# Encoder block on one core: bias products over 128 rows, the two last banks added by halves in turns, and sums moved in VectorE's queue

## The chip, the cores and the metric

The kernel runs on one core of a Trainium2 chip. The metric is the time of one execution on the device, in microseconds (us); less is better. The executions shown are few, so the median is given with the lowest and the highest. One further execution was recorded by the profiler, and all rows quoted below come from that one.

## The reference

The kernel computes one encoder block for one sequence of 256 tokens with 2048 channels in float32. Three token mixers (A: six heads of dilated windows with a relative bias; B: grouped queries with rotary positions; C: cross-attention into 256 memory tokens) run beside each other on one projection, each is sent through its own matrix and gated, and the sum goes through an output projection. A feed-forward part with 5632 hidden channels follows.

```python
h = rms_norm(x, g_mix)
qa, ka, va, qb, kb, vb, qc, gt = split(h @ w_in)
# per dilation group: scores + rel_bias[t5_bucket(rel)] inside the window, NEG outside
oa = mixture of the three dilated groups, by their softmax denominators
ob, oc = grouped-query attention, cross-attention into rms_norm(mem)
merged = sigmoid(gt)[0]*(oa @ w_br_a) + sigmoid(gt)[1]*(ob @ w_br_b) + sigmoid(gt)[2]*(oc @ w_br_c)
x = x + merged @ w_o
hf = rms_norm(x, g_ffn) @ w_ffn_in
return x + (silu(hf[..., :D_FF]) * hf[..., D_FF:]) @ w_ffn_out
```

## The kernel before

**Products.** Tokens stand in two tiles of 128 (t = 0, 1). A float32 product is made of three float32r matmuls: each weight chunk (128x1024, called `raw`, `more` or `both` after the place where SyncE's DMA put it) is rounded by ScalarE to `whi` (L457), VectorE subtracts to get the rest `wlo` (L468), and TensorE adds x_hi·whi, x_hi·wlo and x_lo·whi into one PSUM bank of 128x512. The three names occur in this order in the rows, so a late `wlo` holds TensorE at the second matmul of a group. In the queue of an engine instructions run strictly in order.

**Blocks.** Behind the attention, `pair` multiplies two column blocks at a time by a scheme with seven block products in place of eight; the banks are called X, Y, V, W and Q after their products. It needs sums of weight chunks (VectorE, L593 to L599 and L662 to L666), sums of banks (L636, L640) and sums of token tiles (`forms`, and for a single chunk `glone` and `lone`). The strings `STEPS_...` list the order of the steps; a step is one chunk, "." gives a turn to nothing. `run` issues each chunk's products four chunks behind its halves.

**Side jobs.** Everything that is not a product (attention, gating, transposes, stores) is a generator in a list; `tick`, called after each step, moves at most one job that is due, and `hold(n, ...)` starts a job n ticks later. An instruction handed to `nc.follow` keeps its place in program order on its engine; matmuls and SyncE's DMAs always do; for the others a scheduler, which plays the program through in its own model of time, decides the order within an engine. So a moved job moves instructions on VectorE, and in the attention part the scheduler may place everything anew when one operation changes its shape.

**Places that the change touches.** `biases` (L406 to L437) makes the tables of the relative bias: a one-hot table of 33 used rows, padded to 64, is loaded (`oneh`), copied to float32r (`ones`), and multiplied with the bias values repeated over columns (`rep`, split to `reps`): three times two matmuls `bias_ps`, with 64 rows of contraction. It runs beside the projections of the attention heads (`product`, names `mm`). `merging` is the stage that gates the branches; in its first pair `lone_of_gates` (L963 on) builds the token sum `glone` on VectorE and ScalarE, and `merge` (its products are L1002) multiplies a branch's two banks with their gates. `feeding` is the feed-forward part; `output` (its sums are L1123) adds banks to x and stores them. The last column block of all is added in halves of 256 columns: token tile 0 (bank mmY) first gets all its products, then token tile 1 (bank mmX) gets its products for the first half of the columns, then for the second half.

Of the kernel before, what the change touches and what calls it, by code (L numbers as in the profile page):

```python
# [104 lines left out]
def encoder_block(ctx: ExitStack, tc: tile.TileContext, a: dict, out: bass.AP):  # L105
# [271 lines left out]
    def constants():  # L377
# [3 lines left out]
        nc.sync.dma_start(out=rope, in_=a["rope"])  # L381
        nc.vector.memset(relb[:64], NEG)
        nc.sync.dma_start(out=relb[:BUCKETS], in_=a["rel_bias"])
# [22 lines left out]
    def biases():  # L406
# [5 lines left out]
        for g in range(3):  # L412
            oneh, ones = s4([P, NC], "oneh"), s4([P, NC], "ones", F32R)
            nc.sync.dma_start(out=oneh[:64], in_=a["onehot"][:, g])
            yield 3
            nc.scalar.activation(ones[:64], oneh[:64], AF.Copy)
            rep = small.tile([P, P], F32, name="rep", bufs=1)
            reps = small.tile([P, 2, P], F32R, name="reps", bufs=1)
            for i in range(2):
                nc.vector.tensor_copy(rep[:64, 64 * i:64 * i + 64],  # L420
                                      relb[:64, 2 * g + i:2 * g + i + 1].to_broadcast([64, 64]))
            ps = bank("bias_ps")
            split(reps[:64, 0], reps[:64, 1], rep[:64])
            for i in range(2):
                nc.tensor.matmul(ps, lhsT=reps[:64, i], rhs=ones[:64], start=(i == 0), stop=(i == 1))
            row = s4([P, RELS], "row")
# [43 lines left out]
    def pair(src, lhs, lists, done, doubles=(), forms=None, operand=None, fresh="", early=False, by_halves=None, single=None):  # L470
# [51 lines left out]
        def whole(u, c):  # L522
            def ready():
# [15 lines left out]
                def products():  # L539
                    halved = by_halves is not None and c == 0 and left[ends[0][1]] == 2  # L540
                    for i in range(2 * T):
                        t, k = (i % T, i // T) if parts == 2 else (i // 2, i % 2)
                        st = at(2 * u + k, t)
                        if not (halved and t):
                            mul(ends[c][t], st, hi[:, k], lo[:, k], parts == 2)
                    for i in range(4 * halved):
                        if i == 2:
                            with tc.high_priority():
                                by_halves([ps[b] for b in ends[0]])
                        st, k = at(2 * u + i % 2, 1), i % 2  # L550
                        mul(ends[0][1], st, hi[:, k], lo[:, k], cols=slice(i // 2 * NC // 2, (i // 2 + 1) * NC // 2),
                            whole_half=i % 2 == 1)
                    ending()
# [409 lines left out]
    def lone_of_gates():  # L963
        yield 18
        to = lone["gate"] = s8([P, 1, 2, 4, P], "glone", pool=tail)
        one, tl = s4([P, 1, 4, P], "ffull"), xT.tiles[2].bitcast(F32)
        nc.vector.tensor_add(one[:, 0].rearrange("p (k t) s -> p k (t s)", t=T), tl[:, :2, 0], tl[:, :2, 1])
        yield 2
        token_sums(one, to)

    def merging():
# [5 lines left out]
        for b, (g0, k0, k1) in enumerate(((0, 0, 2), (8, 2, 6), (4, 6, 12))):  # L977
            for j in (0, 2) if b else (2,):
                sg, br = {}, {}

                def gates(c, r, j=j, b=b, sg=sg, br=br):
                    sg[c] = s4([P, T, NC], "sg")
                    for t in range(T):
                        nc.scalar.activation(sg[c][:, t], r[t], AF.Sigmoid, scale=r_x[:, 0, t:t + 1])
                    if c in br:
                        start(hold(11 if b < 2 else 0, merged(c, [br[c][:, t] for t in range(T)], j, b, sg)))

                def branch(c, r, j=j, b=b, sg=sg, br=br):
                    if c in sg:
                        return merge(c, r, j, b, sg)  # L990
                    br[c] = s4([P, T, NC], "br")
                    for t in range(T):
                        nc.scalar.activation(br[c][:, t], r[t], AF.Copy)

                def merged(c, r, j, b, sg):
                    merge(c, r, j, b, sg, nc.follow if b < 2 else lambda ins: None)
                    yield 1

# [88 lines left out]
    def feeding():  # L1087
        for c0, c1 in ((0, 4), (4, 8), (8, KF // 4)):
# [25 lines left out]
            for n in (0, 2):  # L1114
                def output(c, r, n=n, last=last, first=False):
                    final = last and n == 2 and c == 0
                    w = NC // 2 if final else NC
                    for t in range(T):
                        for h in range(NC // w):
                            if final and first != (t + h < 2):  # L1120
                                continue
                            o = slice((n + c) * NC + h * w, (n + c) * NC + (h + 1) * w)
                            nc.vector.scalar_tensor_tensor(x[t][:, o], r[t][:, h * w:(h + 1) * w],  # L1123
                                                           r_f[:, 0, t:t + 1], x[t][:, o],
                                                           op0=ALU.mult, op1=ALU.add)
                            if last:
                                start(hold(1 if n else 4, store(t, o)))

                yield pair(lambda u, c, n=n, c0=c0: a["w_ffn_out"][n + c][2 * c0 + u], hTl, pairs[n // 2], output,
                           TWO, by_room(lambda: room), by_halves=(lambda r, f=output: f(0, r, first=True)) if last and n == 2 else None)  # L1130

# [19 lines left out]
def _onehot():  # L1151

    m = np.zeros((64, 3, NC), np.float32)
    for g, (radius, dil) in enumerate(DILS):
# [67 lines left out]
```

## Time and profile before

| | |
|---|---|
| median of 3 executions | 1356.69 us (1356.67 to 1357.27) |
| the profiled execution's own time | 1357.38 us |
| its span (first to last instruction) | 1355.6 us |
| granted TensorE clock | 1.00 |
| busy: TensorE matmul, VectorE, ScalarE | 99%, 87%, 64% |
| mean busy share of the DMA engines over 40 slices | between 0.2 and 0.9 |

A row of the timeline gives the start (us from the span's start), the time taken, engine, line, operation, output<-inputs, how many equal ones were merged, and in brackets how long the engine had been idle and what ended that. PE is TensorE's matmuls, PEld its weight loads, DVE VectorE, ACT ScalarE. Ends of matmuls are modelled: one 128x512 matmul is shown with 0.39 us, while the next one starts about 0.23 us after it. So TensorE's lost time is read from the distance between starts, not from the busy share.

### The profile page before, as it was taken

The numbers are of one execution on the slowest core, as the hardware profiler recorded it, in microseconds if no ns is written. First come the engines' busy times: TensorE is split into PE (matmuls) and PEld (weight loads), VectorE is DVE, ScalarE is ACT, GpSimd is POOL, SyncE is SP. The second block draws the span as 40 slices with busy tenths as digits, with TensorE's granted clock in tenths as the row PEclk, the third lists the DMA queues.
The fourth block names the chain that finished last, engine by engine and source line by source line (L and its number), as shares of the span: only waits on it lengthen the run. The fifth ranks groups of instructions, "written<-read, shape, count | busy, mean of one in ns | idle before, by whom it ended". The sixth has DMA issues, their size and how long they took to land.

```text
span 1355.6 us, 17347 instructions
## 1 busy us (share of the span) xinstructions
PE 1348.8 (99%) x6156; PEld 1117.9 (82%) x6156; DVE 1176.5 (87%) x1458; ACT 864.7 (64%) x1136; POOL 53.1 (4%) x60
## 2 busy tenths in 40 slices
PE   9999999999999999999999999999999999999998
PEld 7888888888888888888888888888888888888887
DVE  6869877768989879889999998988999888989997
ACT  7877665655666656657766666655667655566663
POOL 0010000000000000000000000000000000000000
PEclk9999999999999999999999999999999999999999
DMA  9976445558495584775568766678666787666872
GB/s 371 346 232 217 144 154 177 165 164 285 187 308 161 174 302 155 281 248 167 190 218 264 242 193 221 209 255 276 191 216 210 240 264 219 220 224 206 279 217 94
DMA packets 86344, 301.19 MB, mean 222 GB/s; under 512 B 9777, under 2 KB 12337, under 8 KB 86001
## 3 DMA queue, kind: packets, MB, share of 16 engines
q1 hardware_dynamic: 79488, 275.94, 57.4%
q0 software_dynamic: 6624, 24.12, 9.6%
q8 instruction: 48, 0.79, 0.2%
q14 instruction: 40, 0.32, 0.1%
q10 hardware_dynamic: 144, 0.02, 0.0%
HBM read 297.17 MB, written 2.88 MB: 221 GB/s over the span
## 4 chain that ended last, share of the span: by engine, by line
PE 96%; DVE 3%; issue 0%; ACT 0%; DMA 0%; SPq 0%; DVEq 0%; ACTq 0%
PE mmX L80 28%; PE mmW L80 20%; PE mm L80 17%; PE mmY L80 15%; PE mmQ L80 11%; DVE wlo L468 2%; PE tp L80 1%; PE sc L80 1%; PE o L80 1%; PE pT L80 1%; PE mmV L80 1%; PE hT L80 0%; DVE raw L666 0%; DMA raw<-in_w_mem 0%; DVE x L1123 0%
## 5 line engine op out<-in xcount | busy, mean ns | idle before, releaser
L457 ACT ACTIVATE whi<-raw 128x1024 fp32r<-128x1024 f32 (+1 forms) x354 | 361.4, 1036 | 218.6 <-DVE raw L666 50.4
L468 DVE TENSOR_TENSOR wlo<-raw,whi 128x1024 fp32r<-128x1024 f32 (+1 forms) x354 | 418.4, 1194 | 65.1 <-ACT whi L457 61.1
L80 PE MATMUL mm<-whi,xT 128*128 128x512 f32 x640 | 201.3, 392 | 0.0
L457 ACT ACTIVATE whi<-both 128x1024 fp32r<-128x1024 f32 (+1 forms) x117 | 117.9, 1015 | 62.1 <-PE mmQ L80 21.9
L468 DVE TENSOR_TENSOR wlo<-both,whi 128x1024 fp32r<-128x1024 f32 (+1 forms) x117 | 136.1, 1170 | 22.6 <-ACT whi L457 21.6
L457 ACT ACTIVATE whi<-more 128x1024 fp32r<-128x1024 f32 (+1 forms) x103 | 106.7, 1038 | 55.0 <-DVE more L664 18.1
L133 DVE TENSOR_TENSOR wlo<-raw,whi 128x1024 fp32r<-128x1024 f32 x82 | 103.1, 1261 | 41.1 <-ACT whi L133 36.3
L80 PEld LDWEIGHTS mm<-whi,xT 128*128 128x128 f32 x640 | 119.3, 188 | 23.4
L468 DVE TENSOR_TENSOR wlo<-more,whi 128x1024 fp32r<-128x1024 f32 (+1 forms) x103 | 123.2, 1198 | 13.5 <-ACT whi L457 12.8
L133 ACT ACTIVATE whi<-raw 128x1024 fp32r<-128x1024 f32 x82 | 87.0, 1062 | 61.6 <-PE mm L80 49.5
L80 PE MATMUL mm<-wlo,xT 128*128 128x512 f32 x320 | 125.6, 392 | 0.0
L80 PE MATMUL mmW<-whi,forms 128*128 128x512 f32 x368 | 122.0, 390 | 0.0
L80 PE MATMUL mmX<-whi,forms 128*128 128x512 f32 x368 | 122.0, 390 | 0.0
L80 PE MATMUL mmX<-whi,x1T 128*128 128x512 f32 x352 | 120.9, 389 | 0.0
L80 PE MATMUL mmY<-whi,x1T 128*128 128x512 f32 x264 | 89.1, 389 | 0.0
L80 PEld LDWEIGHTS mmW<-whi,forms 128*128 128x128 f32 x368 | 69.1, 188 | 14.2
L80 PEld LDWEIGHTS mmX<-whi,forms 128*128 128x128 f32 x368 | 69.1, 188 | 14.2
L80 PEld LDWEIGHTS mmX<-whi,x1T 128*128 128x128 f32 x352 | 66.1, 188 | 13.7
L80 PE MATMUL mmX<-wlo,forms 128*128 128x512 f32 x184 | 71.8, 390 | 0.2 <-DVE wlo L468 0.2
L80 PE MATMUL mmW<-wlo,forms 128*128 128x512 f32 x184 | 71.6, 389 | 0.0
L80 PEld LDWEIGHTS mm<-wlo,xT 128*128 128x128 f32 x320 | 60.1, 188 | 12.4 <-issue 0.7
L80 PE MATMUL mmX<-wlo,x1T 128*128 128x512 f32 x176 | 68.5, 389 | 0.0
(311 smaller groups left out, 2602.0 us busy)
## 6 DMA issues: line engine op xcount, KB each, us to landing
raw<-in_w_ffn SPq DMA_DIRECT2D x109, 512.0 KB, 7.4
raw<-in_w_qkv SPq DMA_DIRECT2D x64, 512.0 KB, 4.2
raw<-in_w_gate SPq DMA_DIRECT2D x58, 512.0 KB, 5.2
raw<-in_w_ffn_out SPq DMA_DIRECT2D x53, 512.0 KB, 7.1
both<-in_w_ffn SPq DMA_DIRECT2D x34, 512.0 KB, 6.2
more<-in_w_ffn SPq DMA_DIRECT2D x33, 512.0 KB, 6.4
both<-in_w_gate SPq DMA_DIRECT2D x24, 512.0 KB, 8.3
raw<-in_w_o SPq DMA_DIRECT2D x24, 512.0 KB, 5.8
```

Of the source, the lines that this page charges most:

```text
L80: ins = op(*args, **kw)
L133: ins = [nc.scalar.activation(hi, src, AF.Copy), nc.vector.tensor_sub(lo, src, hi.bitcast(F32))]
L457: nc.follow(nc.scalar.activation(hi[:, o], v, AF.Copy))
L468: nc.follow(nc.vector.tensor_sub(*part))
```

## The change

Five things are edited. The one-hot tables, the repeated bias values and the six bias matmuls use all 128 rows (the added rows of the table are zero). In the last chunk's products, both banks are filled by halves of columns, and the halves take turns: tile 0 first half, tile 1 first half, tile 0 second half, tile 1 second half; each half is added to x and stored after its own products. The job for `glone` starts at tick 22 in place of 18. The gated products of the first block in `branch` start ten ticks later and keep their program order. The sums for column block 0 of the last feed-forward output (`late`) are made seven ticks later and keep program order, and their stores move with them.

```diff
@@ constants, biases
-        nc.vector.memset(relb[:64], NEG)
+        nc.vector.memset(relb, NEG)
...
-            nc.sync.dma_start(out=oneh[:64], in_=a["onehot"][:, g])
+            nc.sync.dma_start(out=oneh, in_=a["onehot"][:, g])
...
-            nc.scalar.activation(ones[:64], oneh[:64], AF.Copy)
+            nc.scalar.activation(ones, oneh, AF.Copy)
...
-                nc.vector.tensor_copy(rep[:64, 64 * i:64 * i + 64],
-                                      relb[:64, 2 * g + i:2 * g + i + 1].to_broadcast([64, 64]))
+                nc.vector.tensor_copy(rep[:, 64 * i:64 * i + 64],
+                                      relb[:, 2 * g + i:2 * g + i + 1].to_broadcast([P, 64]))
...
-            split(reps[:64, 0], reps[:64, 1], rep[:64])
+            split(reps[:, 0], reps[:, 1], rep)
...
-                nc.tensor.matmul(ps, lhsT=reps[:64, i], rhs=ones[:64], start=(i == 0), stop=(i == 1))
+                nc.tensor.matmul(ps, lhsT=reps[:, i], rhs=ones, start=(i == 0), stop=(i == 1))
@@ pair, whole, products
-                    for i in range(2 * T):
+                    for i in range(2 * T * (not halved)):
                         t, k = (i % T, i // T) if parts == 2 else (i // 2, i % 2)
-                        st = at(2 * u + k, t)
-                        if not (halved and t):
-                            mul(ends[c][t], st, hi[:, k], lo[:, k], parts == 2)
-                    for i in range(4 * halved):
-                        if i == 2:
-                            with tc.high_priority():
-                                by_halves([ps[b] for b in ends[0]])
-                        st, k = at(2 * u + i % 2, 1), i % 2
-                        mul(ends[0][1], st, hi[:, k], lo[:, k], cols=slice(i // 2 * NC // 2, (i // 2 + 1) * NC // 2),
-                            whole_half=i % 2 == 1)
+                        mul(ends[c][t], at(2 * u + k, t), hi[:, k], lo[:, k], parts == 2)
+                    for i in range(2 * T * halved):
+                        t, h = i % T, i // T
+                        for k in range(2):
+                            mul(ends[0][t], at(2 * u + k, t), hi[:, k], lo[:, k],
+                                cols=slice(h * NC // 2, (h + 1) * NC // 2), whole_half=k == 1)
+                        with tc.high_priority():
+                            by_halves(ps[ends[0][t]], t, h)
+                    if halved:
+                        ended.add(0)
@@ lone_of_gates
-        yield 18
+        yield 22
@@ merging
-                        start(hold(11 if b < 2 else 0, merged(c, [br[c][:, t] for t in range(T)], j, b, sg)))
+                        start(hold(0 if b == 2 else 11, merged(c, [br[c][:, t] for t in range(T)], j, b, sg,
+                                                                     b < 2, (1,))))
...
                     if c in sg:
-                        return merge(c, r, j, b, sg)
+                        return start(hold(0 if c else 10, merged(c, r, j, b, sg, not c)))
@@ feeding
-                def output(c, r, n=n, last=last, first=False):
...
+                def add(bank, t, c0, w, pace, n=n, last=last, place=lambda ins: None):
+                    o = slice(c0, c0 + w)
+                    place(nc.vector.scalar_tensor_tensor(x[t][:, o], bank, r_f[:, 0, t:t + 1], x[t][:, o],
+                                                         op0=ALU.mult, op1=ALU.add))
+                    if last:
+                        start(hold(pace, store(t, o)))
+
+                def output(c, r, n=n, last=last, add=add):
+                    late = last and n == 0 and c == 0
+
+                    def adding():
+                        for t in range(T):
+                            add(r[t], t, (n + c) * NC, NC, 1 if n else 4, place=nc.follow if late else lambda ins: None)
+                        yield from ()
+                    start(hold(7 if late else 0, adding()))
+
+                def quarter(bank, t, h, n=n, add=add):
+                    add(bank[:, h * NC // 2:(h + 1) * NC // 2], t, n * NC + h * NC // 2, NC // 2, 1)
```

What this does to the order within an engine is shown at three places, as differences of the two programs' instruction lists (- before, + with the change; a number behind a name tells buffers apart, and the line numbers 1002 and 1123 became 1003 and 1118). The first is VectorE in the first pair of `merging`; the operations that make `glone` are ffull (L967), fraw (L353 to L355) and glone itself (L133).

```order
-L967 TENSOR_TENSOR ffull<-xT 128x512
-L468 TENSOR_TENSOR wlo<-both,whi 128x1024
-L353 TENSOR_TENSOR fraw<-ffull 128x256
+L468 TENSOR_TENSOR wlo<-both,whi 128x1024
 L627 TENSOR_TENSOR mmV<-mmV,u 128x512
 L640 TENSOR_TENSOR mmQ<-m_3409,mmX 128x512
 L666 TENSOR_TENSOR raw_3345<-raw_3326,raw_3345 128x1024
 L468 TENSOR_TENSOR wlo<-both,whi 128x1024
-L354 TENSOR_TENSOR fraw<-fraw,ffull 128x128
```

The first two operations for `glone` leave the place ahead of the second `wlo<-both`; the five come back 8 to 12 rows of the list later than before, spread among other work, the last one (L133) between the two gated products of block 1.

The second is VectorE about 40 us later, at the end of the same pair's first phase; mg is the merged sum, mmY and mmX hold the branch's block 0, and sg its gates.

```order
 L636 TENSOR_TENSOR mmW<-m_3777,mmX 128x512
 L664 TENSOR_TENSOR raw_3587<-raw_3585,raw_3587 128x1024
-L1002 TENSOR_TENSOR mg_2849<-mmY,sg 128x512
 L468 TENSOR_TENSOR wlo<-both,whi 128x1024
 L597 TENSOR_TENSOR raw_3592<-raw_3590,raw_3592 128x512
-L1002 TENSOR_TENSOR mg_2850<-mmX,sg 128x512
 L468 TENSOR_TENSOR wlo<-raw_3587,whi 128x1024
 L468 TENSOR_TENSOR wlo<-raw_3592,whi 128x512
 L468 TENSOR_TENSOR wlo<-raw_3590,whi 128x512
```

Both gated products leave this place and stand 14 and 16 rows further on, behind L599 and one more `wlo<-both`.

The third is the end of the program: TensorE's last matmuls, where mmY is token tile 0 and mmX token tile 1 of the last column block.

```order
 L80 MATMUL mmX<-wlo,hT 128x256
-L80 MATMUL mmX<-whi,hT 128x256 x2
+L80 MATMUL mmX<-whi,hT 128x256
+L80 MATMUL mmY<-whi,hT 128x256
+L80 MATMUL mmY<-wlo,hT 128x256
+L80 MATMUL mmY<-whi,hT 128x256 x2
+L80 MATMUL mmY<-wlo,hT 128x256
+L80 MATMUL mmY<-whi,hT 128x256
+L80 MATMUL mmX<-whi,hT 128x256
 L80 MATMUL mmX<-wlo,hT 128x256
```

Between the two halves of mmX there now stand six matmuls of 256 columns for the second half of mmY; ahead of the first half of mmX, mmY gets six of 256 columns in place of six of 512. On VectorE, in the last 30 us, the two sums for column block 0 (x<-mmY, x<-mmX, L1123) leave the place behind L636 and stand 10 rows later, ahead of the last three `wlo`; in the attention part (about 90 to 210 us) single rows of PE, DVE and ACT change places by a few rows.

More of the change, by code (lines that the diff above doesn't have):

```diff
@@ L993, in branch, with merged @@
                         nc.scalar.activation(br[c][:, t], r[t], AF.Copy)
-                def merged(c, r, j, b, sg):
-                    merge(c, r, j, b, sg, nc.follow if b < 2 else lambda ins: None)
-                    yield 1
+                def merged(c, r, j, b, sg, inline, rest=()):
+                    merge(c, r, j, b, sg, nc.follow if inline else lambda ins: None)
+                    yield from rest
                 def merge(c, r, j, b, sg, place=lambda ins: None):
@@ L1114, in feeding @@
             for n in (0, 2):
-                def output(c, r, n=n, last=last, first=False):
[L1116 to L1127, printed above, removed]
+                def add(bank, t, c0, w, pace, n=n, last=last, place=lambda ins: None):
[13 more added lines that the diff above has]
+                    add(bank[:, h * NC // 2:(h + 1) * NC // 2], t, n * NC + h * NC // 2, NC // 2, 1)
                 yield pair(lambda u, c, n=n, c0=c0: a["w_ffn_out"][n + c][2 * c0 + u], hTl, pairs[n // 2], output,
-                           TWO, by_room(lambda: room), by_halves=(lambda r, f=output: f(0, r, first=True)) if last and n == 2 else None)
+                           TWO, by_room(lambda: room), by_halves=quarter if last and n == 2 else None)
     def everything():
@@ L1151, in _onehot @@
 def _onehot():
-    m = np.zeros((64, 3, NC), np.float32)
+    m = np.zeros((P, 3, NC), np.float32)
     for g, (radius, dil) in enumerate(DILS):
```

## Prediction

> **What bounds the kernel.** I read the page first.
>
> ```profile
> PE 1348.8 (99%) x6156; PEld 1117.9 (82%) x6156; DVE 1176.5 (87%) x1458; ACT 864.7 (64%) x1136; POOL 53.1 (4%) x60
> ```
>
> TensorE is the bound, so a change can save only what TensorE loses, and the busy share hides it. The chain of waits shows the pace without loss, and the list of waits for TensorE shows who makes it wait.
>
> ```profile
> 1172.00 4.08 PE mmX L80 x18
> ...
> PE mmX L80 <- DVE x L1123: 0.7, 1, 0.7
> PE mmW L80 <- DVE wlo L468: 0.4, 1, 0.4
> ```
>
> Eighteen matmuls of 128x512 take 4.08 us: one starts every 0.227 us. The list shows little waiting, since it counts from the modelled end of the matmul before. I therefore went through the timeline for starts further apart than 0.227. Behind the start-up I find four kinds of place that this change touches, all with VectorE as the releaser or with the bias products in them. They are the terms below.
>
> **The bias products, 128 rows.**
>
> ```profile
> L80 PE MATMUL bias_ps<-ones,reps 64*128 64x512 f32 x6 | 2.2, 443 | 0.0
> ...
> 91.70 0.61 PE L80 MATMUL mm<-whi,xT 128*128 128x512 f32 x2
> 92.24 0.73 PE L80 MATMUL bias_ps<-ones,reps 64*128 64x512 f32 x2
> 92.90 0.50 PE L80 MATMUL mm<-wlo,xT 128*128 128x512 f32 x1
> 93.24 0.62 PE L80 MATMUL mm<-whi,xT 128*128 128x512 f32 x2
> ```
>
> The second matmul of the first row of the timeline starts at 91.93. From there to 93.24 are four intervals in 1.31 us, where 4 x 0.227 = 0.91 is the pace: 0.40 lost around one pair, before, inside and behind it. These six are the program's only matmuls of 64 rows, and there are three pairs: 3 x 0.40 = 1.2. With 128 rows they have the shape of their neighbours, and I take the whole 1.2. No row shows a 128-row bias product, so the bounds are 0 (the loss comes from something else there) and 1.3. What it adds is hidden: the copies keep their number of columns and stand on engines that TensorE doesn't wait for here, and three tables of 256 KB in place of 128 KB are loaded well ahead of their use (the last rival weighs that).
>
> The Trainium skill speaks on both sides here. "TensorEngine Tiling (Array Packing)", Key Properties, says that a change of the tiling mode drains TensorE; by it the gain is the full 1.2, and the four long intervals agree. "TensorE: Matmul & The Clock Gate", Part 2, Step-by-step, says that the number of rows doesn't matter to a weight load; by it alone the edit would save 0 and the kernel would come out at 1354.4.
>
> **The token sum at tick 22.**
>
> ```profile
> 331.85 0.68 DVE L967 TENSOR_TENSOR ffull<-xT 128x512 f32<-128x512 f32 x1
> ...
> 336.25 1.21 DVE L468 TENSOR_TENSOR wlo<-both,whi 128x1024 fp32r<-128x1024 f32 x1
> ...
> 337.05 0.39 PE L80 MATMUL mmW<-whi,xT 128*128 128x512 f32 x1
> 337.52 0.50 PE L80 MATMUL mmW<-wlo,xT 128*128 128x512 f32 x1
> 337.86 0.62 PE L80 MATMUL mmW<-whi,xT 128*128 128x512 f32 x2
> ```
>
> TensorE's second start comes 0.47 after the first (0.24 lost, for the rest of 1.21 us of subtraction that ends at 337.46), and the next one 0.34 later (0.11 more: after each such wait the first interval is long). That is 0.35. VectorE's queue ahead of the late `wlo` holds L967, which occupies it for 0.60 (as any sum of 128x512, below: 373.12 to 373.72), and L353. Without L967 alone the `wlo` ends at 336.86, and TensorE asks for it at 337.05 + 0.23 = 337.28. The stall goes: 0.35, and 0.4 us are spare.
>
> **The gated products and the stalls behind them.**
>
> ```profile
> 352.46 1.29 DVE L468 TENSOR_TENSOR wlo<-raw,whi 128x512 fp32r<-128x512 f32 x2 [1.64 <-ACT whi L457]
> ...
> 365.64 1.23 DVE L468 TENSOR_TENSOR wlo<-raw,whi 128x1024 fp32r<-128x1024 f32 x1 [0.20 <-ACT whi L457]
> ...
> 370.79 0.68 DVE L1002 TENSOR_TENSOR mg<-mmY,sg 128x512 f32<-128x512 f32 x1
> ...
> 373.12 0.68 DVE L1002 TENSOR_TENSOR mg<-mmX,sg 128x512 f32<-128x512 f32 x1
> 373.72 3.55 DVE L468 TENSOR_TENSOR wlo<-raw,whi 128x1024 fp32r<-128x1024 f32 x4
> ...
> 374.14 0.61 PE L80 MATMUL mmX<-whi,forms 128*128 128x512 f32 x2
> 374.99 0.50 PE L80 MATMUL mmX<-wlo,forms 128*128 128x512 f32 x1 [0.23 <-DVE wlo L468]
> ...
> 379.47 1.21 DVE L468 TENSOR_TENSOR wlo<-both,whi 128x1024 fp32r<-128x1024 f32 x1
> 380.34 0.39 PE L80 MATMUL mmW<-whi,xT 128*128 128x512 f32 x1
> 380.74 0.50 PE L80 MATMUL mmW<-wlo,xT 128*128 128x512 f32 x1
> ```
>
> Two stalls stand here. The second matmul of the row at 374.14 starts at 374.37 and the next at 374.99: 0.62 - 0.23 + 0.11 = 0.50. The one at 380.34 loses 0.40 - 0.23 + 0.11 = 0.28.
>
> Leaving VectorE's queue ahead of 373.72 are both gated products, each 0.60 (373.12 to 373.72): 1.20 earlier. Entering it, at 350 to 359, are the five operations for `glone`. Of these the first (0.60) falls into the idle 1.64 ahead of 352.46. The last (0.60) stands in a stretch without idle time. Three small ones (128x256 and twice 128x128, together as many columns as one of 128x512) lie behind short idle times in which VectorE waits for ScalarE and for the branch's banks. I take 0.60 for the last and 0.07 for the small ones that isn't hidden: VectorE is 0.67 later. Bounds are 0.60 (all of the small ones hidden) and, as an estimate, 0.94 (about half of them hidden). The idle 0.20 at 365.64 doesn't absorb it, as I expect ScalarE, its releaser, to be pushed back by VectorE's earlier sums. The net is 1.20 - 0.67 = 0.53 earlier. Then `wlo` starts at 373.19 and ends 1.22 later, at 374.41, while TensorE asks for it at 374.60: the 0.50 goes, by a margin of 0.19.
>
> At 380 both have moved: VectorE's `wlo` ends at 380.68 - 0.53 = 380.15, and TensorE, 0.50 earlier, asks at 380.57 - 0.50 = 380.07. With the 0.06 that lies between the end of a `wlo` and TensorE's start (337.46 to 337.52) the wait is 0.14 + 0.11 = 0.25, where it was 0.28. So **what is late next is the same engine 6 us later**, and the pair of stalls gives 0.53. Bounds: with VectorE 0.94 late, the first wait keeps 0.25 and the pair gives 0.25; with 0.60 it gives 0.57, and 0.78 if both vanish. The gated products land where VectorE's next needs are not near; their banks are asked for again only by a later pair.
>
> **The sums of column block 0.**
>
> ```profile
> 1328.47 0.74 DVE L1123 SCALAR_TENSOR_TENSOR x<-mmY,scales,x 128x512 f32<-128x512 f32 x1
> 1329.13 0.74 DVE L1123 SCALAR_TENSOR_TENSOR x<-mmX,scales,x 128x512 f32<-128x512 f32 x1
> ...
> 1336.58 0.39 PE L80 MATMUL mmW<-whi,hT 128*128 128x512 f32 x1
> 1337.33 0.50 PE L80 MATMUL mmW<-wlo,hT 128*128 128x512 f32 x1 [0.37 <-DVE wlo L468]
> ```
>
> Here 0.75 - 0.23 + 0.11 = 0.63 is lost to a `wlo` behind both sums, each of which occupies VectorE for 0.66. Without them it comes 1.32 earlier, and half of that would do. The stall goes: 0.63. The sums come back ahead of the last three `wlo`; SyncE's stores move behind the last four weight loads, which are thereby issued no later than before.
>
> ```profile
> 1340.92 1.23 DVE L468 TENSOR_TENSOR wlo<-more,whi 128x1024 fp32r<-128x1024 f32 x1
> 1344.26 0.39 PE L80 MATMUL mmX<-wlo,hT 128*128 128x512 f32 x1
> ```
>
> The first `wlo` behind them ends at 1342.15 and is used at 1344.26. It keeps the 1.32 that it gained, loses 1.32 again, and TensorE is 0.63 earlier: 1.5 spare. If that cover were gone, 1.32 would be the price.
>
> **Halves in turns.**
>
> ```profile
> 1348.12 0.39 PE L80 MATMUL mmY<-whi,hT 128*128 128x512 f32 x1
> ...
> 1349.48 0.28 PE L80 MATMUL mmX<-whi,hT 128*128 128x256 f32 x1
> ...
> 1350.07 0.28 PE L80 MATMUL mmX<-whi,hT 128*128 128x256 f32 x1
> 1350.47 0.47 DVE L1123 SCALAR_TENSOR_TENSOR x<-mmX,scales,x 128x256 f32<-128x256 f32 x1
> 1351.00 0.39 PE L80 MATMUL mmX<-whi,hT 128*128 128x256 f32 x1 [0.65 <-DVE x L1123]
> ...
> 1351.70 0.28 PE L80 MATMUL mmX<-whi,hT 128*128 128x256 f32 x1
> 1352.02 0.48 DVE L1123 SCALAR_TENSOR_TENSOR x<-mmX,scales,x 128x256 f32<-128x256 f32 x1 [1.07 <-PE mmX L80]
> ```
>
> TensorE's second half of a bank waits until VectorE has read the first half. From the unit's first matmul to the last start are 1351.70 - 1348.12 = 3.58. Now: six matmuls of 256 columns from 0, the last at 0.59, the next six from 0.70 to 1.29. VectorE starts 0.32 after a half's last start (1351.70 to 1352.02) and takes 0.48: mmY's first half is read by 1.39. TensorE may go on at 1.45 (0.06 later), where it would have wanted 1.41. With a wait's long interval (the six from 1351.00 to 1351.70) mmY's last start is 2.15; mmX's first half is read by 2.09, no wait; mmX runs from 2.26 to 2.85. The gain is 3.58 - 2.85 = 0.73, and the last sum and store follow as before. Bounds: 0 if each half waits for both sums ahead, 0.83 with no wait at all.
>
> **Sum.** 1.2 + 0.35 + 0.53 + 0.63 + 0.73 = 3.44. Against the profiled execution's 1357.38 that is 1353.94; that execution lies 0.69 above the median, and I take the difference over: 1356.69 - 3.44 = 1353.25, said as 1353.2.
>
> **Rivals.** *The rows are not what costs.* The long intervals stay, because they belong to the short run of other matmuls and not to 64 rows: 1353.2 + 1.2 = 1354.4. Against it stands that the six are the only ones of this shape and that the loss begins and ends with them; for it, that the trace has no bias product of another shape to compare. Chance 0.13.
>
> *VectorE stays the bound in the merging stage.* The `glone` work costs more than 0.67 there: 1353.5 at 0.94, and 1353.75 if the pair of stalls gives nothing. The margin is only 0.19. Chance 0.16.
>
> *A new wait in the attention part.* The scheduler has moved single transposes and score products by up to six matmuls of 0.227 us, most of them later. One that now stands ahead of its producer costs up to that: 1354.0 to 1354.6. The list of waits names none for TensorE in that part today. Chance 0.09.
>
> *Slower: the doubled one-hot table.* ScalarE's queue is strict and waits for that load already.
>
> ```profile
> oneh<-in_onehot SPq DMA_DIRECT2D x3, 128.0 KB, 4.4
> ...
> 95.96 0.63 ACT L416 ACTIVATE ones<-oneh 64x512 fp32r<-64x512 f32 x1 [2.16 <-DMA oneh<-in_onehot]
> ...
> 99.92 0.73 PE L80 MATMUL bias_ps<-ones,reps 64*128 64x512 f32 x2
> ```
>
> The copy ends at 96.59 and is used at 99.92: 3.3 spare. A load that takes longer than 4.4 + 3.3 = 7.7 us holds TensorE, us for us; to end 0.2% slower it must take 7.7 + 3.4 + 2.7 = 13.8 us, and the time would be 1359.4. Twice the bytes at an unchanged rate would be 8.8: 1.1 us lost, 1354.3. Chance 0.02 for slower.
>
> **Chances.** The forecast, all five terms near their size, 0.60, with its own range 1352.7 to 1353.9. About 0.2% (2.7 us, below 1354.0) is what a measurement of this kernel can tell from no change. Faster by more: 0.58 of the forecast and 0.15 of the second rival, 0.73. Within it: the rest of these, the first and the third rival, 0.25. Slower: 0.02. The range from 1352.6 to 1354.7 takes in the first three rivals and leaves out some 0.15.
>
> **What would show it.** In the changed profile the bias rows should be `128x512` at 0.227 us apart, the starts at about 336.6, 373.5 and 1334 should be on pace, a wait of 0.1 to 0.3 should be left near 379, and the last unit should take 2.85 us from first to last start. The forecast is wrong if the bias intervals stay at 0.32, if VectorE's `wlo` near 373 ends later than TensorE's call, or if TensorE waits anywhere between 90 and 320.

## The result, and the profile after

The changed kernel takes 1354.53 us, median of 20 runs (1354.12 to 1355.65), beside 1357.19 for the kernel before in 20 runs on the same chip. The ratio is 0.9981, with a 95% interval from 0.9974 to 0.9987: 2.7 us less (1.8 to 3.5 by the interval), where 3.44 was predicted. The median of 1354.53 lies above the forecast's own range (1352.7 to 1353.9) and inside the wider one that takes in its rivals (to 1354.7). One execution among all the runs below, of the kernel `only_halves`, took 2769 us, twice the others' time; why is not known, and no ratio uses it. The profiled execution of the changed kernel takes 1354.21 us and spans 1352.4 of them; that of before took 1357.38 and spanned 1355.6.

The page of the changed kernel has the same bound, and its list of waits for TensorE is short:

```profile
PE 1346.8 (100%) x6162; PEld 1117.8 (83%) x6162; DVE 1176.0 (87%) x1458; ACT 864.1 (64%) x1136; POOL 53.1 (4%) x60
...
PE mmY L80 <- ACT whi L457: 0.3, 1, 0.3
PE mmW L80 <- DVE wlo L468: 0.2, 1, 0.2
```

TensorE is still busy for all of the span, so again only the distances between starts tell what is lost. The timeline of TensorE at the places of the prediction, and VectorE's last sum (start, duration, engine, line, operation, output<-inputs, shape, idle time before it):

```profile
85.88 0.48 PE L80 MATMUL mm<-whi,xT 128*128 128x512 f32 x1
...
92.33 0.61 PE L80 MATMUL bias_ps<-ones,reps 128*128 128x512 f32 x2
92.78 0.39 PE L80 MATMUL mm<-wlo,xT 128*128 128x512 f32 x1
...
336.15 0.39 PE L80 MATMUL mmW<-whi,xT 128*128 128x512 f32 x1
336.38 0.39 PE L80 MATMUL mmW<-wlo,xT 128*128 128x512 f32 x1
...
372.87 0.62 PE L80 MATMUL mmX<-whi,forms 128*128 128x512 f32 x2
373.33 0.40 PE L80 MATMUL mmX<-wlo,forms 128*128 128x512 f32 x1
...
378.59 0.39 PE L80 MATMUL mmW<-whi,xT 128*128 128x512 f32 x1
378.89 0.50 PE L80 MATMUL mmW<-wlo,xT 128*128 128x512 f32 x1
379.23 0.64 PE L80 MATMUL mmW<-whi,xT 128*128 128x512 f32 x2
...
1334.76 0.39 PE L80 MATMUL mmW<-whi,hT 128*128 128x512 f32 x1
1334.99 0.39 PE L80 MATMUL mmW<-wlo,hT 128*128 128x512 f32 x1
...
1345.64 0.28 PE L80 MATMUL mmY<-whi,hT 128*128 128x256 f32 x1
...
1347.10 0.39 PE L80 MATMUL mmY<-whi,hT 128*128 128x256 f32 x1
1347.32 0.28 PE L80 MATMUL mmY<-wlo,hT 128*128 128x256 f32 x1
...
1348.51 0.28 PE L80 MATMUL mmX<-whi,hT 128*128 128x256 f32 x1
1348.83 0.48 DVE L1118 SCALAR_TENSOR_TENSOR x<-mmX,scales,x 128x256 f32<-128x256 f32 x1 [0.23 <-PE mmX L80]
```

All the places read as the prediction said, but for a slightly smaller stall at 379. The bias pair goes through at the pace of 0.227 (92.33 to 92.78 for two). The stall at 337 is gone: 336.15 to 336.38 is on pace. So is the first one of the merging stage: the matmuls that stood at 374.37 and 374.99 before start at 373.10 and 373.33. The second is smaller: 0.30 and 0.34, which loses 0.19 where 0.25 was expected. The stall of the last stage is gone (1334.76 to 1334.99). The last unit takes 1348.51 - 1345.64 = 2.87, predicted 2.85, with one long interval of 0.22 at 1347.10.

To see where the time went, take the start of one and the same matmul in both traces. The row of before for the first of these places is

```profile
85.71 0.48 PE L80 MATMUL mm<-whi,xT 128*128 128x512 f32 x1
```

and the others stand in the prediction (337.05, 380.34, 1336.58, and 1352.02 for VectorE's last sum).

| up to | before | after | shift | gained since the place above | predicted |
|---|---|---|---|---|---|
| after the memory stage | 85.71 | 85.88 | +0.17 | -0.17 | 0 |
| merging, first product | 337.05 | 336.15 | -0.90 | 1.07 (bias) | 1.20 |
| the second stall | 380.34 | 378.59 | -1.75 | 0.85 (token sum, first stall) | 0.85 |
| last stage, `mmW` | 1336.58 | 1334.76 | -1.82 | 0.07 (second stall) | 0.03 |
| last sum | 1352.02 | 1348.83 | -3.19 | 1.37 (sums, halves) | 1.36 |

In the two profiled executions, then, the terms behind the start-up are right to 0.13 each, and 0.17 is lost ahead of all that the change touches in TensorE's order. (0.08 of the bias term's 0.13 is one interval at 113.24, in the scores of the attention part, that is longer than its neighbours; more on that place below.) But the medians differ by 2.66 and not by 3.19, and that is what the experiments had to explain.

### The profile page after: what moved, and what is told of

Read it like the earlier page. It is cut to its first block, busy times and chain, and to the rows that moved or that the text cites. A ratio compares the mean times of both kernels' runs of the same rounds, so it can differ in the third digit from the quotient of the medians.

```text
span 1352.4 us, 17360 instructions
## 1 busy us (share of the span) xinstructions
PE 1346.8 (100%) x6162; PEld 1117.8 (83%) x6162; DVE 1176.0 (87%) x1458; ACT 864.1 (64%) x1136; POOL 53.1 (4%) x60
## 4 chain that ended last, share of the span: by engine, by line
PE 97%; DVE 1%; DMA 0%; ACT 0%; issue 0%; SPq 0%; ACTq 0%
PE mmX L80 29%; PE mmW L80 21%; PE mm L80 17%; PE mmY L80 15%; PE mmQ L80 11%; PE tp L80 1%; PE sc L80 1%; PE o L80 1%; DVE wlo L468 1%; PE mmV L80 1%; PE pT L80 1%; PE hT L80 0%; DMA raw<-in_w_mem 0%; ACT whi L457 0%; PE bias_ps L80 0%
## 5 line engine op out<-in xcount | busy, mean ns | idle before, releaser
L133 DVE TENSOR_TENSOR wlo<-raw,whi 128x1024 fp32r<-128x1024 f32 x82 | 103.2, 1262 | 36.2 <-ACT whi L133 31.1
L133 ACT ACTIVATE whi<-raw 128x1024 fp32r<-128x1024 f32 x82 | 87.1, 1063 | 59.2 <-PE mm L80 48.8
```

The lines of the kernel that those rows point to most:

```text
L133: ins = [nc.scalar.activation(hi, src, AF.Copy), nc.vector.tensor_sub(lo, src, hi.bitcast(F32))]
```

## The experiments

**One part at a time.** Four kernels are the kernel before with one part of the change each, and a fifth has the halves alone. Shifts below are against the first trace of before, at the same matmul. By the medians alone none of these five can be told from no change: each 95% interval takes in 1. So what each part does is read from the distances within its trace.

`only_bias`: the bias products and their tables.

```diff
-            nc.sync.dma_start(out=oneh[:64], in_=a["onehot"][:, g])
+            nc.sync.dma_start(out=oneh, in_=a["onehot"][:, g])
...
-                nc.tensor.matmul(ps, lhsT=reps[:64, i], rhs=ones[:64], start=(i == 0), stop=(i == 1))
+                nc.tensor.matmul(ps, lhsT=reps[:, i], rhs=ones, start=(i == 0), stop=(i == 1))
...
```

> The kernel before with the bias products over 128 rows and nothing else of the change. Theory (matmuls of 64 rows among those of 128 cost some 0.10 us at each of four intervals): at the three pairs the intervals go from 0.32-0.34 to 0.227, all that follows starts 1.2 us earlier, and the profiled run takes 1356.2 in place of 1357.38. Rival (the long intervals belong to any short run of other products): they stay at 0.32, and the run takes 1357.4. Second question, the 0.17 us that the changed kernel starts its stage behind the memory stage later than the one before: if the wider memset or table does it, it is here too; if it is chance in the first loads, it is not bound to any part.

Measured: 1356.40 us, 0.99 below the median of before beside it (ratio 0.9993, interval 0.9983 to 1.0002). The start-up has next to no shift (0.01), all three pairs are on pace, and from 180 up to the last stage everything starts 1.08 to 1.15 earlier. The twelve long intervals held 1.22; 0.09 comes back as one long interval more in the attention part, where single operations stand in another order. The profiled execution took 1355.90, 0.3 less than expected: the stall near 1336 is 0.38 shorter here than in the first trace, which `only_sums` below comes back to. The first theory holds, and the 0.17 at the start is not seen in this kernel, which has the wider tables too.

`only_token`: the token sum.

```diff
-        yield 18
+        yield 22
```

> The kernel before with the token sum at tick 22 and nothing else. Theory (VectorE is the bound from 350 to 375, so what is taken from 332 is paid again there): the stall at 337.05 goes (-0.35), but VectorE reaches the subtractions of 373.72 some 0.67 later while TensorE asks 0.35 earlier, so the stall at 374.37 grows from 0.50 to about 1.5; net 0.7 slower, profiled run about 1358.0. Rival (the idle time of VectorE near 350 and 365 takes all of it up): the stall at 374 grows by 0.35 only, net 0, 1357.4. Second rival (the moves are independent): net -0.35, 1357.0.

Measured: 1357.33, ratio 0.9999 (0.9989 to 1.0009), not to be told from no change. In the trace the five operations for `glone` stand 11 to 17 places later on VectorE (not 8 to 12, as said above). Up to 345 the shift falls from +0.49 (start-up) to +0.08, which is the stall at 337 gone; by 380 it is back at +0.71. This is its timeline of TensorE there, with two stalls in place of one:

```profile
373.09 0.39 PE L80 MATMUL mmX<-whi,forms 128*128 128x512 f32 x1
373.95 0.50 PE L80 MATMUL mmX<-wlo,forms 128*128 128x512 f32 x1 [0.47 <-DVE wlo L468]
374.29 0.63 PE L80 MATMUL mmX<-whi,forms 128*128 128x512 f32 x2
...
374.98 0.63 PE L80 MATMUL mmX<-whi,forms 128*128 128x512 f32 x2
375.69 0.49 PE L80 MATMUL mmX<-wlo,forms 128*128 128x512 f32 x1
```

So alone this part pays back what it takes, and 0.2 more: less than the 0.7 of the theory, more than the 0 of the rival. The figure of 0.7 was an error of its own: it let TensorE run 0.35 earlier from 337 on and left VectorE where it was. VectorE waits for ScalarE and for TensorE's banks near 350 (the idle time in the prediction's rows), so it moves along. Against TensorE it is 0.61 later behind the token sum, close to the 0.67 of the prediction.

`only_gated`: the gated products held.

```diff
-                        return merge(c, r, j, b, sg)
+                        return start(hold(0 if c else 10, merged(c, r, j, b, sg, not c)))
...
```

> The kernel before with the gated products held ten steps and nothing else. Theory: VectorE is 1.20 earlier at 373.72, so the stalls at 374.37 (0.50) and at 380.34 (0.28) both go, the one at 337.05 (0.35) stays; profiled run 1356.6. Rival (the products land where they hold the next subtraction, 386 on, or a bank that TensorE wants): a new wait behind 385, and 0.5 or less is left of the gain, 1356.9 or later.

Measured: 1356.52, 0.87 below the median of before (ratio 0.9994, 0.9985 to 1.0003). Both stalls are gone and no new one stands behind 385; the shift goes from +0.36 to -0.49, a gain of 0.85, where 0.78 was expected. In its timeline the place of 374 and that of 380 are on pace:

```profile
373.37 0.39 PE L80 MATMUL mmX<-whi,forms 128*128 128x512 f32 x1
373.60 0.39 PE L80 MATMUL mmX<-wlo,forms 128*128 128x512 f32 x1
...
380.17 0.39 PE L80 MATMUL mmW<-whi,xT 128*128 128x512 f32 x1
380.40 0.39 PE L80 MATMUL mmW<-wlo,xT 128*128 128x512 f32 x1
```

The two parts don't add: the token sum alone costs about 0.2 (0.49 to 0.70), the products alone give 0.85, and both give 0.92 (0.85 + 0.07 in the table). What is left at 379 in the changed kernel is the price of the token sum's new place.

`only_sums`: the sums of column block 0.

```diff
+                    if late:
+                        start(hold(7, adding()))
...
```

> The kernel before with the sums of column block 0 of the last stage held seven steps and nothing else. Theory: the wait at 1336.58 goes whole, 0.63, and nothing comes back before the end; profiled run 1356.75. Rival (the sums or their stores hold the last loads or the last subtractions): a part of 1.32 comes back behind 1341, 1356.9 or later.

Measured: 1357.11, only 0.28 below the median of before (ratio 0.9999, 0.9990 to 1.0009). The stall is gone whole, and nothing comes back: against the first trace of before the shift goes from +0.17 to -0.48. But the median gains less than half of that. A likely reason lies in the trace of the kernel before. In the three kernels above, which leave this place as it was, the stall near 1336 is not 0.63 but 0.25. `only_gated`:

```profile
1336.12 0.39 PE L80 MATMUL mmW<-whi,hT 128*128 128x512 f32 x1
1336.48 0.50 PE L80 MATMUL mmW<-wlo,hT 128*128 128x512 f32 x1
1336.82 0.40 PE L80 MATMUL mmW<-whi,hT 128*128 128x512 f32 x1
```

Here 0.36 and 0.34 lose 0.25. VectorE's stream shows where the two executions part. Row by row, VectorE in the trace of before is 0.46 behind that of `only_gated` from 1280 to 1320, as TensorE is, and 0.85 behind from 1322.19 on. The row of ScalarE that feeds it there, in before and then in `only_gated` (whose row holds two copies; the second, at 1320.07, is the one that starts at 1321.09 in before):

```profile
1321.09 2.01 ACT L457 ACTIVATE whi<-raw 128x1024 fp32r<-128x1024 f32 x2 [0.47 <-DMA raw<-in_w_ffn_out]
```

```profile
1319.10 2.01 ACT L457 ACTIVATE whi<-raw 128x1024 fp32r<-128x1024 f32 x2 [0.83 <-DVE raw L662]
```

And VectorE's next subtraction in before:

```profile
1322.19 1.23 DVE L468 TENSOR_TENSOR wlo<-raw,whi 128x1024 fp32r<-128x1024 f32 x1 [0.31 <-ACT whi L457]
```

In the first profile a weight load came late: it landed 5.2 us after its issue, 4.2 in `only_gated` and 4.3 to 4.7 in `only_token`, `only_bias` and `only_halves`. ScalarE waited 0.47 for it, and VectorE, which has no idle time at this place in `only_gated`, waited 0.31 for ScalarE. From there VectorE is 0.39 later and works without a gap up to the subtraction that TensorE waits for at 1336, so TensorE's stall is 0.38 longer. The term of 0.63 was that of one execution. That the usual stall of before is 0.25 is argued from other kernels that have this place unchanged; a second profile of before is not there.

`only_halves`: the last two banks by halves in turns.

```diff
+                        for k in range(2):
+                            mul(ends[0][t], at(2 * u + k, t), hi[:, k], lo[:, k],
+                                cols=slice(h * NC // 2, (h + 1) * NC // 2), whole_half=k == 1)
...
```

> The kernel before with both last banks added by halves in turns and nothing else. Theory: the last unit, from its first to its last matmul start, goes from 3.58 to 2.85, and the median is 0.73 below that of before, 1356.65. Rival (the extra store order or VectorE's sums hold the end): the last start is 0.73 earlier but the span ends less than 0.5 earlier. Besides, a question on the stall near 1336, which was 0.63 in the first profile of before and 0.25 in three later profiles of kernels that leave this place as it was: if a late weight load ahead of it made the difference, it is 0.25 here where ScalarE shows no wait for a load near 1321, and 0.6 where it does.

Measured: 1356.46, 0.83 below the median of before (ratio 0.9994, 0.9985 to 1.0004). The last unit takes 2.87 from first to last start, as in the changed kernel. Against the first trace of before its first start is 0.23 earlier, by the shorter stall near 1336, its last start 0.94 and the end of the span 0.95 earlier; so the rival fell. Near 1321 ScalarE waits for no load, and that stall is 0.25: the fourth execution of this kind against one.

**What a 64-row product costs.** Both are the changed kernel with other bias products.

```diff
-                nc.tensor.matmul(ps, lhsT=reps[:, i], rhs=ones, start=(i == 0), stop=(i == 1))
+                nc.tensor.matmul(ps, lhsT=reps[:96, i], rhs=ones[:96], start=(i == 0), stop=(i == 1))
```

> The changed kernel with bias products that read the first 96 rows in place of all 128 (the rows left out are zero in the table). Theory A (what costs is that a product uses half of the array's rows, another mode of it): 96 rows stay in the mode of 128, and all intervals are 0.227, as in the changed kernel. Theory B (any product that leaves rows of the array out is loaded without overlap): four intervals of 0.32-0.34 at each pair, 1.1 us lost again, profiled run about 1355.3.

```diff
-            for i in range(2):
-                nc.tensor.matmul(ps, lhsT=reps[:, i], rhs=ones, start=(i == 0), stop=(i == 1))
+            for i in range(4):
+                nc.tensor.matmul(ps, lhsT=reps[:64, i % 2], rhs=ones[:64], start=(i % 2 == 0), stop=(i % 2 == 1))
```

> The changed kernel with bias products of 64 rows again, each pair computed twice over (four matmuls in a row, the second pair overwrites the first). Theory A (the change of mode costs, at its two ends): the loss per group stays at 0.40, the intervals inside the group are 0.227. Theory B (each matmul of 64 rows and the two starts behind the last one cost 0.10): 0.60 per group, all intervals inside at 0.32. The two extra matmuls cost 0.45 per group besides.

Their timelines at the first group, `rows96` and then `four64`:

```profile
91.50 0.62 PE L80 MATMUL mm<-whi,xT 128*128 128x512 f32 x2
91.96 0.63 PE L80 MATMUL bias_ps<-ones,reps 96*128 96x512 f32 x2
92.43 0.39 PE L80 MATMUL mm<-wlo,xT 128*128 128x512 f32 x1
```

```profile
91.40 0.61 PE L80 MATMUL mm<-whi,xT 128*128 128x512 f32 x2
91.94 1.20 PE L80 MATMUL bias_ps<-ones,reps 64*128 64x512 f32 x4
93.07 0.50 PE L80 MATMUL mm<-wlo,xT 128*128 128x512 f32 x1
93.41 0.63 PE L80 MATMUL mm<-whi,xT 128*128 128x512 f32 x2
```

Two products of 96 rows take 0.47, next to the pace of 0.45; so do those of the second pair. (In the third, the two are 0.33 apart, and a weight load there had waited 0.26 for VectorE's `headT`: that belongs to the wait shown below.) Of 64 rows, the starts from 91.63 are 0.318, 0.335, 0.235, 0.234, 0.323 and 0.342 apart: the two starts behind each change of shape are long, those in the middle are not, and the loss is 0.43 for four products, where it was 0.41 for two. `four64` took 1356.65 us in its one execution. Theory A holds in both. The Trainium skill, "TensorEngine Tiling (Array Packing)", Key Properties, has it that changing the tiling mode drains TensorE; these traces agree and put some 0.2 us on each change. It is a cost of the change of shape at 64 rows, not of fewer rows as such.

`rows96` took 1354.54 us in its one execution, no less than the changed kernel, although its start-up was 0.37 shorter. That was lost here:

```profile
112.86 0.39 PE L80 MATMUL mm<-wlo,xT 128*128 128x512 f32 x1
113.56 0.62 PE L80 MATMUL sc<-headT 128*128 128x256 f32 x3 [0.31 <-DVE headT L133]
```

A wait in the attention part, as the third of the prediction's rivals has it, is there in this execution: 0.70 - 0.23 = 0.47 at this place, with a long interval on each side of it. But its cause is nearer to the fourth rival, the larger one-hot table.

**What holds TensorE at 113.** ScalarE's rows for the third copy of the one-hot table, in before, in the changed kernel and in `rows96`:

```profile
106.31 0.63 ACT L416 ACTIVATE ones<-oneh 64x512 fp32r<-64x512 f32 x1 [1.94 <-DMA flat<-row]
```

```profile
109.36 0.63 ACT L416 ACTIVATE ones<-oneh 128x512 fp32r<-128x512 f32 x1 [4.31 <-DMA flat<-row]
```

```profile
109.71 0.63 ACT L416 ACTIVATE ones<-oneh 128x512 fp32r<-128x512 f32 x1 [4.95 <-DMA flat<-row]
```

The copy is 3.0 us later than before, and ScalarE stands idle for it, with the `headT` of the next scores behind it in its strict queue. By the profile the last thing that it waits for is the store of the row before, which is issued right behind the table's load and, in the changed kernel, lands 0.7 us after it. SyncE's queue shows why both are late, in before and in the changed kernel:

```profile
100.74 0.49 SPq L80 DMA_DIRECT2D oneh<-in_onehot  x1
101.33 0.52 SPq L80 DMA_DIRECT2D flat<-row  x1
```

```profile
100.46 2.18 SPq L80 DMA_DIRECT2D raw<-in_w_qkv  x2
102.73 0.38 SPq L80 DMA_DIRECT2D oneh<-in_onehot  x1
103.20 0.38 SPq L80 DMA_DIRECT2D flat<-row  x1
```

There is now a second weight load ahead of the third table, so the store is issued 1.9 later; from its issue to the copy are 4.98 us before and 6.16 now. The table itself is issued 2.0 later and takes 5.8 us to land in place of 4.0, so it lands 3.9 later (the 1.8 in the expectation below is the longer transfer alone). In the first profile of the changed kernel TensorE lost only 0.08 at 113; in `rows96` the table took 6.5 and the store 6.7 us, the copy is 0.35 later, TensorE earlier, and it waits. The test takes the larger load away and zeroes the other rows with GpSimd, products unchanged:

```diff
-            nc.sync.dma_start(out=oneh, in_=a["onehot"][:, g])
+            nc.sync.dma_start(out=oneh[:64], in_=a["onehot"][:64, g])
+            nc.gpsimd.memset(oneh[64:], 0.0)
```

> The changed kernel with the one-hot tables loaded with 64 rows as before, the other 64 rows of the tile set to zero by GpSimd; products stay at 128 rows. Theory (in the changed kernel the third table's load is issued 2 us later and lands 1.8 us later than before, ScalarE waits 4.3 us for it in place of 1.9, and the scores at 113 start with next to no spare time, so a slow load holds TensorE): the third copy starts near 106.5 in place of 109.4, no wait at 113 whatever the start-up, the executions of 1355.1 to 1355.7 (5 of 20 of the changed kernel) are gone, median 1354.2 or less. Rival (those executions come from the first loads of the program): as many of them remain, median 1354.5.

> The changed kernel once more, beside half_load, for the spread. Theory of the third load: median 1354.4 to 1354.7, about a quarter of the executions above 1355; in the profile a wait of TensorE near 113 if the start-up was shorter than in the first profile or the third load longer. Rival: no wait near 113 in this profile either, and the same spread in half_load.

Measured side by side: `half_load` 1353.93 (1353.50 to 1354.89, 8 runs; ratio to before 0.9975, 0.9965 to 0.9986), the changed kernel again 1354.30 (1354.04 to 1355.93, 11 runs; 0.9979, 0.9970 to 0.9988). In `half_load` the attention part is in the order of before. ScalarE's row in `half_load`:

```profile
107.74 0.63 ACT L417 ACTIVATE ones<-oneh 128x512 fp32r<-128x512 f32 x1 [2.21 <-DMA flat<-row]
```

Its start-up is 0.88 longer than that of before, so against TensorE the copy is back to within 0.55 of its old place (107.74 - 0.88 = 106.86, was 106.31), and there is no wait at 113. Against the first trace of the changed kernel it starts 0.71 later at 86 and 0.53 later from 180 on: 0.18 is gained in the attention part, the 0.08 at 113 and one long interval. The second profile of the changed kernel has no wait at 113 either; its start-up was 0.13 longer than in the first, and its median of 1354.30 is just below what the theory gave for it. The fastest execution of `half_load` is 0.54 below the fastest of the changed kernel. That speaks for the theory of the third load, but two things weaken it: the intervals of the two ratios overlap, and the edit takes away both the larger load and the new order, so what each of them costs isn't told apart. Of the executions above 1355 there were 5 of 20 and 1 of 11 in the changed kernel, none of 8 in `half_load`; with so few that is no proof of where they come from, and it stays open.

**The stalls that are left.** Both kernels lose 0.36 near 540, where a `wlo` stands behind four operations of VectorE, two gated products and two sums of them.

```diff
-                        start(hold(0 if b == 2 else 11, merged(c, [br[c][:, t] for t in range(T)], j, b, sg,
+                        start(hold(0 if b == 2 else 16, merged(c, [br[c][:, t] for t in range(T)], j, b, sg,
```

> The changed kernel with the hold of the gated products of the second branch at sixteen steps in place of eleven, which puts four operations of VectorE behind two subtractions that TensorE waits for near 539 (0.36 lost there in both kernels). Theory (VectorE's queue is what is late there too): that stall goes, 0.36, 1354.2 against the changed kernel's 1354.5. Rival (the operations behind them, a token sum and its split, are late next, or transposes that need the sums): the stall moves by some microseconds and nothing or less is gained.

Measured: 1354.35 (ratio 0.9980, 0.9971 to 0.9990), not to be told from the changed kernel. The stall at 539 is gone, and the rival holds: the transposes, which read the moved sums, are late next.

```profile
543.11 0.30 PE L80 MATMUL tp<-ident,mg 128*128 128x128 f32 x1
543.62 0.55 PE L80 MATMUL tp<-ident,mg 128*128 128x128 f32 x3 [0.21 <-DVE mg L1009]
```

Two starts 0.51 apart, where 0.11 is the pace of transposes; with the intervals around them 0.6 is lost. The last kernel is `half_load` with this hold, and with the transposes moved too:

```diff
-                            yield {0: 5, 2: 2}.get(j + c, 4)
+                            yield {0: 7, 2: 2}.get(j + c, 4)
```

> half_load, with the hold of sixteen steps of later16 and the transposes of the first column block of the merged sums two steps later. Theory (what later16 lost at 543 was transposes that wait for sums that stand behind the subtractions): neither the stall at 539 (0.36) nor the one at 543 (0.6); median 0.36 below half_load, about 1353.8. Rival (the later transposes are waited for by the product that reads them, at 556 and on): a new wait there of up to 2 us, no gain.

Measured: 1353.34 (1353.05 to 1353.69, 6 runs; ratio to before 0.9970, 0.9958 to 0.9981). The place of 539 is on pace:

```profile
538.63 0.39 PE L80 MATMUL mmW<-whi,xT 128*128 128x512 f32 x1
538.86 0.39 PE L80 MATMUL mmW<-wlo,xT 128*128 128x512 f32 x1
```

No wait of TensorE is left between 530 and 560, and none has come in behind. Its median is the lowest of all kernels here, 0.6 below `half_load` beside it, where 0.36 was expected; the intervals of the two overlap. In the two traces the difference is 1.34, but 0.81 of it is the start-up; 0.53 is gained behind that, 0.44 of it between 530 and 543.

## Why the prediction was right, and where it was off

The direction and the mechanism of all five terms were right; the size of the whole was too large by 0.35 to 0.8 (3.44 against 2.66 in the first comparison and 3.09 in the later one; the first one's interval, 1.8 to 3.5, just takes in 3.44). The time itself was 1.3 above the 1353.2 forecast. 0.8 of that is the gain, and 0.5 is the kernel before, whose median is 1357.19 in 20 executions and was 1356.69 in the three that the prediction started from. The chances put 0.73 on a time below 1354.0 and 0.25 on one within 2.7 us of the kernel before; it was the second. By its own steps:

- **Bias products, 1.20.** All twelve long intervals went. 1.07 arrived in the changed kernel, 1.08 to 1.15 alone. The rival (the rows are not what costs, but the short run of other matmuls) fell with `only_bias`, where the same short runs of 128 rows are on pace; `rows96` and `four64` add that 64 rows cost through the change of shape.
- **Token sum, 0.35.** The stall went. By itself the move is worth nothing, since VectorE then is late at 374; the prediction had this 0.67 in the next term, where `only_token` shows 0.61 and the changed kernel 0.62.
- **Gated products and the stalls behind, 0.53.** 0.59 by the intervals: 0.50 gone, 0.28 down to 0.19. "What is late next is the same engine 6 us later" held. The rival of VectorE staying the bound fell. (By the prediction's own steps the pair gives 0.60 at VectorE 0.60 late, where it says 0.57; the sum doesn't use that bound.)
- **Sums of column block 0, 0.63.** This is the term that was mis-sized. The prediction took the whole 0.63 as the price of VectorE's two sums. The sums' move takes the stall away, but 0.38 of the 0.63 came from one late weight load in the profiled execution of before; in four profiled executions of other kernels with this place unchanged it is 0.25, and the median of `only_sums` is 0.28 lower. The row `[0.47 <-DMA raw<-in_w_ffn_out]` stood in the trace 15 us ahead of it and wasn't followed back.
- **Halves in turns, 0.73.** 0.71 in the traces (3.58 to 2.87), in the changed kernel and alone. (The bound with no wait at all is 0.89 by the prediction's figures, 3.58 less four runs of 0.59 and three steps of 0.11, where it says 0.83.)
- **From one execution to the median.** The prediction took the difference of the profiled executions over to the median. The first profile of before had a short start-up as well as a long stall at 1336, so it was no mean of its kernel in either.

With 0.38 less for the fourth term the gains of the table are 1.07 + 0.85 + 0.07 + 0.99 = 2.98, between the two measured differences. What is left between 2.66 and 2.98 is not shown to have one cause. A part may be the third table: the rival on the doubled one-hot load priced its second copy, which had 3.3 us to spare. The third has next to none, because the load also moved behind another one in SyncE's queue. It was this copy whose row should have been looked up. The medians of the two comparisons of the same kernels differ by 0.43 between themselves, so a rest of 0.3 may be no more than spread.

## What to carry to other kernels

A stall read from one trace has the size of that execution. Before it goes into a sum, follow the engine that makes TensorE wait back to the last place where that engine itself waited; if this is a DMA, the stall can have another size in the next execution, as 0.63 and 0.25 here. When an operation is moved out of a full queue, look for the next place where the queue is full, and move what stands there as well: two moves here gave 0.92 together, 0.85 and -0.2 alone. And matmuls over 64 rows among those of 128 cost time here and saved none; padding them is worth trying if the padded table's load has time to spare.

## What the runs showed that was not expected

The start-up differs by more than a microsecond between executions. The matmul at 85.71 in the first trace of before starts between 85.41 and 86.59 in the thirteen traces, the first in `four64` and the last in `half_load`:

```profile
85.41 0.48 PE L80 MATMUL mm<-whi,xT 128*128 128x512 f32 x1
```

```profile
86.59 0.48 PE L80 MATMUL mm<-whi,xT 128*128 128x512 f32 x1
```

These two programs differ in their first loads, but `both_later`, which is the same program as `half_load` up to there, has this matmul at 85.78, 0.81 earlier. This spread is larger than four of the sum's five terms, and is why the single parts could be told apart only by shifts within one trace. Stalls come and go in the same way: `later16` and `four64` lose 0.31 at 316.5 and 319.0, where the other traces lose nothing, and their change doesn't touch that place. And 96 rows of 128 cost nothing while 64 rows cost 0.4 a group, with two matmuls in the group as with four.
